# A modulation of one or two row vectors, summed on the vector engine instead of multiplied on the tensor engine

## The chip, the cores and the metric

The kernel runs on one core of a Trainium2 chip. The metric is the device time of one execution in microseconds, as the median of several runs. The engines are named as the profile names them: PE is the tensor engine (PEld its weight loads), DVE the vector engine, ACT the scalar engine, POOL the GpSimd engine, and SP issues most of the DMAs.

## The reference, cut to what matters

Two transformer blocks follow one another on 512 tokens of width 1024. The first has a hybrid mixer (dilated attention and retention), a cross attention to 256 memory tokens and a gated MLP. The second block is modulated: six vectors of width 1024 are computed from a condition vector `c`, and the same from `c_ctx` for the context tokens.

```
silu_c = jax.nn.silu(c)[:, None, :]
silu_cc = jax.nn.silu(c_ctx)
mod_x = jnp.split(silu_c @ w_mod[l] + b_mod[l], N_MOD, axis=-1)
mod_c = jnp.split(silu_cc @ w_mod[l] + b_mod[l], N_MOD, axis=-1)
h  = _modulate(_rms(x, norm_attn[l]), mod_x[0], mod_x[1])
hc = _modulate(_rms(ctx, norm_attn[l]), mod_c[0], mod_c[1])
...
x = x + mod_x[2] * _merge(...)
x = x + mod_x[5] * _sq_relu_mlp(_modulate(_rms(x, norm_mlp[l]), mod_x[3], mod_x[4]), w_mlp_in[l], w_mlp_out[l])
```

`w_mod` is 1024 x 6144 in float32, 25 MB. The product is thus two rows of 1024 times this matrix. Of `mod_c` only the first two of the six vectors are used.

## The kernel before, in words

All of it is float32. A large product is made of three products of split operands: ACT rounds a tile to its high part (`whi`, `xhi`), DVE subtracts to get the low part (`wlo`, `xlo`), and TensorE multiplies high by high, high by low and low by high (`mm3s`, lines 227 to 237).

Weights come in tiles of 512 KB (`weights`, lines 153 to 181): four row tiles of 128 by 256 columns. SP issues the load to one of two buffers `wraw` (line 172). Then `step` is called (line 175), then ACT makes `whi` (line 178) and DVE makes `wlo` (line 179), each with two buffers. A product over 1024 rows needs two such tiles, so the two buffers of `whi` and `wlo` hold just one product's weights.

`step` (lines 183 to 189) advances a generator that carries background work for the second block: one step at each weight load, and a second one at each eighth load. The generator is set in `mixer` (line 532), after the projections of the first half of the attention. It is `modulation`, 48 steps, followed by `part_ahead`, 48 steps that split columns of the second block's input weights and store them. Both load through three buffers of 4 KB a partition, named `fraw`, in the pool `fill`.

A step of `modulation` (lines 773 to 781) issues from SP the load of one row tile, 128 rows by 1024 columns, for vector j and row tile k, and then sends the products of the tile that was loaded two steps before. Such products (lines 748 to 755) are four matmuls with the two condition columns as weights, padded to 32 columns; each of the four takes 256 columns and lies in its own 32 columns of the array. They add up over eight row tiles in one PSUM bank of the tag `fl`. At the eighth tile ACT copies the bank, two transposes turn it, and DVE adds the bias to the result in `mods`, where features lie on partitions (lines 756 to 764). For vectors 2 and 5 a further transpose and an ACT DMA store the vector as a row (lines 765 to 771).

`modulation_inputs` (lines 727 to 735) loads the two condition vectors and the bias by ACT's queue and turns them by the helper `rows_T` (lines 706 to 719), each with a buffer of its own.

The steps fall beside this work of the first block: the attention (to about 200 us), the projections of the retention (200 to 265), the keys and values of the memory (`memory`, lines 579 to 602, about 265 to 350, one 512 KB tile of weights for half as much matmul work as in the projections before) and the output projection (from 350). The attention's softmax and the retention's norms need DVE, ACT and POOL.

The order on SP is that of the program. On the other engines a planner orders the instructions by program order and by when it reckons them ready; each engine then runs its list in order.

Of the kernel before, what the change touches and what calls it, by code (L numbers as in the profile page):

```python
# [10 lines left out]
F32 = mybir.dt.float32  # L11
F32R = mybir.dt.float32r
BF = mybir.dt.bfloat16
AF = mybir.ActivationFunctionType
OP = mybir.AluOpType
# [60 lines left out]
class Kernel:  # L76
# [204 lines left out]
    def turned(self, xs, t0, A, B, out, tags):  # L281

        nc = self.nc
        for k in range(8):
            pt = self.bank([128, 2, 128], tags[k % 2])
            for t in range(2):
                nc.tensor.transpose(pt[:, t], xs[t0 + t][:, k * 128:k * 128 + 128], self.ident)
            f = pt.rearrange("p a b -> p (a b)")
            to = [v[:, t0 * 128:t0 * 128 + 256] for v in out(k)]
            if B is None:  # L290
                self.split(*to, f, scale=A[:, k:k + 1])
                continue
            p2, f = f, self.page([256])
            if k % 2:
                nc.scalar.activation(f, p2, AF.Identity, scale=A[:, k:k + 1], bias=B[:, k:k + 1])
            else:
                nc.vector.tensor_scalar(f, p2, A[:, k:k + 1], B[:, k:k + 1], op0=OP.mult, op1=OP.add)
            self.split(*to, f)
# [407 lines left out]
    def rows_T(self, srcs, tag, func=None, eng=None, pool=None):  # L706

        nc = self.nc
        n = sum(k for _, k in srcs)
        r = (pool or self.tmp).tile([128, 128], F32, name="rows" + (tag if pool else "r"), bufs=1)[:n]  # L710
        i = 0
        for src, k in srcs:
            (eng or nc.sync).dma_start(r[i:i + k], bass.AP(tensor=src.tensor, offset=src.offset, ap=[[128, k], [1, 128]]))
            i += k
        if func is not None:
            nc.scalar.activation(r, r, func)
        pt = self.bank([128, n], "pt")
        nc.tensor.transpose(pt, r, self.ident[:n, :n])
        return pt
# [7 lines left out]
    def modulation_inputs(self):  # L727

        nc, ap = self.nc, self.ap
        pt = self.rows_T([(ap["c_2"], 8), (ap["c_ctx_2"], 8)], "crow", AF.Silu, nc.scalar, self.fill)  # L730
        cs = self.fill.tile([128, 8, 32], F32, name="cs")
        nc.gpsimd.memset(cs, 0.0)
        nc.vector.tensor_copy(cs[:, :, :2], pt.rearrange("p (v k) -> p k v", v=2))
        bm = self.cols([(ap["b_mod_2"], 48)], "bmod", self.fill, nc.scalar)
        self.mod_in = cs, bm

    def modulation(self):

        nc, ap = self.nc, self.ap
        cs, bm = self.mod_in
        mods = self.mods = self.const.tile([128, 48, 2], F32, name="mods")
        w = ap["w_mod_2"][0]
        self.modrow = {}
        bank = {}

        def products(j, k, raw):
            if k == 0:
                bank[0] = self.bank([128, 256], "fl")  # L750
            ps = bank[0]
            for q in range(4):
                nc.tensor.matmul(ps[32 * q:32 * q + 32], cs[:, k], raw[:, 256 * q:256 * q + 256], start=k == 0, stop=k == 7, tile_position=(0, 32 * q))
            if k < 7:
                return
            m = self.fill.tile([128, 256], F32, name="fm")
            nc.scalar.activation(m, ps, AF.Copy)
            pt = self.bank([128, 2, 4, 32], "fl")
            for f in range(2):
                nc.tensor.transpose(pt[:, f].rearrange("p a b -> p (a b)"), m[:, f * 128:f * 128 + 128], self.ident)  # L760
            mj = mods[:, 8 * j:8 * j + 8].rearrange("p (q f) v -> p f q v", f=2)
            for f in range(2):
                b = bm[:, 8 * j:8 * j + 8].rearrange("p (q f) -> p f q", f=2)[:, f, :, None].to_broadcast([128, 4, 2])
                nc.vector.tensor_tensor(mj[:, f], pt[:, f, :, :2], b, op=OP.add)
            if j in (2, 5):
                pr = self.bank([8, 128], "fl")
                nc.tensor.transpose(pr, mods[:, 8 * j:8 * j + 8, 0], self.ident)
                r = self.fill.tile([8, 128], F32, name="fr")
                nc.vector.tensor_copy(r, pr)
                d = self.modrow[j] = self.dram.tile([8, 128], F32, name=f"modrow{j}")  # L770
                nc.scalar.dma_start(d, r)

        todo = []
        for j in range(6):
            for k in range(8):
                raw = self.fill.tile([128, 2, 512], F32, name="fraw", bufs=3).rearrange("p a b -> p (a b)")
                nc.sync.dma_start(raw, w[k * 128:k * 128 + 128, j * 1024:j * 1024 + 1024])
                todo.append((j, k, raw))
                if len(todo) > 2:
                    products(*todo.pop(0))  # L780
                yield
        for t in todo:
            products(*t)

    def gain_shift(self, g, sh, sc, v, tag):

        a = self.const.tile([128, 8], F32, name=tag)
        self.nc.vector.scalar_tensor_tensor(a, self.mods[:, sc * 8:sc * 8 + 8, v], 1.0, g, op0=OP.add, op1=OP.mult)
        return a, self.mods[:, sh * 8:sh * 8 + 8, v]
# [805 lines left out]
```

## Time and profile before

| what | us |
|---|---|
| median of 3 runs (2325.2 to 2325.77) | 2325.56 |
| the profiled execution | 2328.74 |
| its span, first to last instruction | 2326.9 |
| PE busy | 2200.2 |
| DVE busy | 1210.9 |
| ACT busy | 965.2 |
| POOL busy | 275.0 |

Durations below come from the one profiled execution. A matmul's busy time is modelled from its start to the end of its pipeline, so the time from one start to the next tells what it takes from the others. A matmul of float32 that isn't split shows as two instructions. Idle time of an engine that isn't the bottleneck costs nothing. The stretches named below are cuts of the span made for this reading.

### The profile page before, as it was taken

How to read it: one execution, taken by the hardware profiler on the slowest of the kernel's cores; microseconds unless marked ns; L12 is line 12 of the kernel's file. 1: busy time of each engine (PE TensorE's matmuls, PEld its weight loads, DVE VectorE, ACT ScalarE, POOL GpSimd, SP SyncE). 2: the span in 40 equal slices, each digit the busy share in tenths (PEclk: the TensorE clock that was granted, in tenths of full speed). 3: DMA queues.
4: the chain of work that ended last, by engine and by line, in shares of the span. 5: the costliest groups of instructions: out<-in, count | busy, mean ns of one | idle time of the engine just before them, and what ended most of it. 6: DMA issues, size and time to landing. Idle time of an engine off the chain costs nothing.

```text
span 2326.9 us, 38350 instructions
## 1 busy us (share of the span) xinstructions
PE 2200.2 (95%) x15415; PEld 1954.7 (84%) x15415; DVE 1210.9 (52%) x2716; ACT 965.2 (41%) x1988; POOL 275.0 (12%) x435
## 2 busy tenths in 40 slices
PE   8999999998989999898989897999999998999999
PEld 8889978897779889777878786888898888898988
DVE  4554444555443333558686867436776354434343
ACT  4442334545333232555555553545655223313221
POOL 0221100001000001201222220202110002010112
PEclk9999999999999999999999998999999998999999
DMA  5234485465762332512121310241012542323332
GB/s 176 83 118 146 161 280 198 137 203 174 234 227 86 99 101 73 179 49 88 46 91 46 97 46 15 73 128 31 29 40 87 181 136 73 100 91 92 99 98 94
DMA packets 195817, 262.06 MB, mean 113 GB/s; under 512 B 12343, under 2 KB 157495, under 8 KB 195639
## 3 DMA queue, kind: packets, MB, share of 16 engines
q1 hardware_dynamic: 188864, 244.61, 32.7%
q10 hardware_dynamic: 6775, 15.00, 1.7%
q8 instruction: 121, 1.98, 0.3%
q14 instruction: 57, 0.47, 0.1%
HBM read 223.39 MB, written 36.18 MB: 112 GB/s over the span
## 4 chain that ended last, share of the span: by engine, by line
PE 74%; issue 9%; DVE 6%; DMA 4%; ACT 4%; POOL 3%; SPq 0%; ACTq 0%; POOLq 0%; DVEq 0%
PE pg L234 15%; PE pg L235 15%; PE pg L237 14%; PE sc L234 4%; PE sc L237 4%; PE sc L235 4%; DMA parts<-fraw 2%; DMA whi<-parts 1%; PE pg L223 1%; PE pg L224 1%; PE pg L225 1%; PE sc L1470 1%; DVE inv L1383 1%; DVE invt L1380 1%; PE pa L1148 1%
## 5 line engine op out<-in xcount | busy, mean ns | idle before, releaser
L179 DVE TENSOR_TENSOR wlo<-wraw,whi 128x1024 fp32r<-128x1024 f32 (+2 forms) x267 | 325.8, 1222 | 407.6 <-ACT whi L178 403.4
L234 PE MATMUL pg<-xhi,whi 128*128 128x512 f32 (+1 forms) x1104 | 426.6, 389 | 27.2 <-DMA whi<-parts 11.3
L178 ACT ACTIVATE whi<-wraw 128x1024 fp32r<-128x1024 f32 (+2 forms) x267 | 275.7, 1035 | 416.9 <-PE pg L235 354.4
L235 PE MATMUL pg<-xlo,whi 128*128 128x512 f32 (+1 forms) x1104 | 425.7, 388 | 0.0
L237 PE MATMUL pg<-xhi,wlo 128*128 128x512 f32 (+1 forms) x1104 | 291.3, 384 | 1.2 <-DMA wlo<-parts 1.0
L234 PEld LDWEIGHTS pg<-xhi,whi 128*128 128x128 f32 x1104 | 210.7, 191 | 73.6 <-ACT whi L178 13.2
L235 PEld LDWEIGHTS pg<-xlo,whi 128*128 128x128 f32 x1104 | 210.9, 192 | 36.7
L237 PEld LDWEIGHTS pg<-xhi,wlo 128*128 128x128 f32 x1104 | 203.1, 190 | 41.1 <-DMA wlo<-parts 2.7
L234 PE MATMUL pg<-whi,xhi 128*128 128x256 f32 (+1 forms) x608 | 158.4, 291 | 0.3 <-ACT a L980 0.3
L235 PE MATMUL pg<-whi,xlo 128*128 128x256 f32 (+1 forms) x608 | 157.2, 289 | 0.0
L234 PE MATMUL sc<-whi,a 128*128 128x256 f32 x560 | 141.5, 285 | 1.6 <-ACT whi L178 1.6
L235 PE MATMUL sc<-whi,a 128*128 128x256 f32 x560 | 141.5, 284 | 0.0
L235 PE MATMUL pg<-whi,a 128*128 128x256 f32 x560 | 140.4, 283 | 0.0
L234 PE MATMUL pg<-whi,a 128*128 128x256 f32 x560 | 140.3, 283 | 0.0
L234 PEld LDWEIGHTS pg<-whi,xhi 128*128 128x128 f32 x608 | 118.4, 195 | 4.7 <-ACT whi L178 2.7
L235 PEld LDWEIGHTS pg<-whi,xlo 128*128 128x128 f32 x608 | 118.1, 194 | 1.1 <-issue 0.8
L237 PE MATMUL pg<-wlo,xhi 128*128 128x256 f32 (+1 forms) x608 | 104.0, 289 | 12.6 <-DVE wlo L179 12.6
L929 POOL TENSOR_TENSOR a<-a,a 128x256 f32<-128x256 f32 x64 | 48.9, 763 | 514.0 <-DVE a L928 513.3
L234 PEld LDWEIGHTS sc<-whi,a 128*128 128x128 f32 x560 | 106.4, 190 | 2.1 <-ACT whi L178 1.8
L1254 DVE SCALAR_TENSOR_TENSOR a<-a,convw,a 128x511 f32<-128x511 f32 (+3 forms) x160 | 100.6, 652 | 13.8 <-ACT a L1248 12.9
L235 PEld LDWEIGHTS sc<-whi,a 128*128 128x128 f32 x560 | 106.2, 190 | 0.3
L234 PEld LDWEIGHTS pg<-whi,a 128*128 128x128 f32 x560 | 105.8, 189 | 0.2
(468 smaller groups left out, 4609.2 us busy)
## 6 DMA issues: line engine op xcount, KB each, us to landing
wraw<-in_w_in SPq DMA_DIRECT2D x56, 512.0 KB, 5.9
fraw<-in_w_mod SPq DMA_DIRECT2D x48, 512.0 KB, 5.5
parts<-fraw SPq DMA_DIRECT2D x48, 512.0 KB, 4.1
wraw<-in_w_gate_up SPq DMA_DIRECT2D x44, 512.0 KB, 4.8
wraw<-in_w_mlp_in SPq DMA_DIRECT2D x32, 512.0 KB, 3.9
wraw<-in_w_mlp_out SPq DMA_DIRECT2D x32, 512.0 KB, 3.4
whi<-parts SPq DMA_DIRECT2D x26, 512.0 KB, 3.9
wlo<-parts SPq DMA_DIRECT2D x26, 512.0 KB
```

The lines of the kernel that those rows point to most:

```text
L178: nc.scalar.activation(hi, raw, AF.Copy)
L179: self.wlo_eng.tensor_tensor(lo, raw, hi.bitcast(F32), op=OP.subtract)
L223: mm(out, a[0], b[0], start=start, stop=False)
L224: mm(out, a[0], b[1], start=False, stop=False)
L225: mm(out, a[1], b[0], start=False, stop=stop)
L234: mm(out, A[k][0], B[k][0], start=start and k == 0, stop=False)
L235: mm(out, A[k][late], B[k][1 - late], start=False, stop=False)
L237: mm(out, A[k][1 - late], B[k][late], start=False, stop=stop and k == n - 1)
L929: nc.gpsimd.tensor_tensor(self.x[t][:, cs], self.x[t][:, cs], u, op=OP.add)
L1148: nc.tensor.transpose(pt[:, s, i * 128:i * 128 + 128], p2[i][:, (2 * s2 + s) * 128:(2 * s2 + s) * 128 + 128], self.ident)
L1254: dve.scalar_tensor_tensor(y, v, wi, y, op0=OP.mult, op1=OP.add)
L1380: dve.tensor_tensor(t_, L[:, j + 1:, j:j + 1].to_broadcast([128, n, w]), Y[:, j:j + 1, b].to_broadcast([128, n, w]), op=OP.mult)
```

## The change

The modulation is computed in another way. The 6144 columns are cut into 24 units of 256. A step loads four row tiles of one unit: still 512 KB, in pieces of 1 KB. DVE multiplies each row tile by the condition's value of each row, a scalar per partition, and adds up the eight row tiles in a tile `facc` (128 by 256). The remaining sum over the 128 partitions is a matmul: `facc` gives the weights, 128 columns at a time, and a column of ones is the moving operand, so that the features come out on partitions with no transpose. The second vector is summed for the first eight units only. A step sends the sums of the tile that was loaded one step before (it was two), and the matmuls of a unit follow one step after its last sums. The rows buffers of condition, bias and a later gain are now one (`rowsf`).

```diff
-        r = (pool or self.tmp).tile([128, 128], F32, name="rows" + (tag if pool else "r"), bufs=1)[:n]
+        r = (pool or self.tmp).tile([128, 128], F32, name="rows" + ("f" if pool else "r"), bufs=1)[:n]
...
-        cs = self.fill.tile([128, 8, 32], F32, name="cs")
-        nc.gpsimd.memset(cs, 0.0)
-        nc.vector.tensor_copy(cs[:, :, :2], pt.rearrange("p (v k) -> p k v", v=2))
+        cs = self.fill.tile([128, 2, 8], F32, name="cs")
+        nc.vector.tensor_copy(cs.rearrange("p v k -> p (v k)"), pt)
+        col = self.fill.tile([128, 1], F32, name="col")
+        nc.gpsimd.memset(col, 1.0)
...
-        def products(j, k, raw):
-            if k == 0:
-                bank[0] = self.bank([128, 256], "fl")
-            ps = bank[0]
-            for q in range(4):
-                nc.tensor.matmul(ps[32 * q:32 * q + 32], cs[:, k], raw[:, 256 * q:256 * q + 256], start=k == 0, stop=k == 7, tile_position=(0, 32 * q))
-            if k < 7:
-                return
-            m = self.fill.tile([128, 256], F32, name="fm")
-            nc.scalar.activation(m, ps, AF.Copy)
-            pt = self.bank([128, 2, 4, 32], "fl")
-            for f in range(2):
-                nc.tensor.transpose(pt[:, f].rearrange("p a b -> p (a b)"), m[:, f * 128:f * 128 + 128], self.ident)
...
+        def of(u):
+            return range(2 if u < 8 else 1)
+
+        def products(u, k0, raw):
+            if k0 == 0:
+                sums[u] = [self.fill.tile([128, 256], F32, name="facc", bufs=3) for v in of(u)]
+            for k in range(k0, k0 + 4):
+                for v, acc in enumerate(sums[u]):
+                    c = cs[:, v, k:k + 1]
+                    if k == 0:
+                        nc.vector.tensor_scalar(acc, raw[:, 0], c, None, op0=OP.mult)
+                    else:
+                        nc.vector.scalar_tensor_tensor(acc, raw[:, k - k0], c, acc, op0=OP.mult, op1=OP.add)
+
+        def turned(u):
+            accs = sums.pop(u)
+            n = len(accs)
+            pt = self.bank([128, 2, n], "fl")
+            for q in range(2):
+                for v in range(n):
+                    nc.tensor.matmul(pt[:, q, v:v + 1], accs[v][:, 128 * q:128 * q + 128], col, start=True, stop=True)
+            b = bm[:, 2 * u:2 * u + 2][:, :, None].to_broadcast([128, 2, n])
+            nc.vector.tensor_tensor(mods[:, 2 * u:2 * u + 2, :n], pt, b, op=OP.add)
...
-        for j in range(6):
-            for k in range(8):
-                raw = self.fill.tile([128, 2, 512], F32, name="fraw", bufs=3).rearrange("p a b -> p (a b)")
-                nc.sync.dma_start(raw, w[k * 128:k * 128 + 128, j * 1024:j * 1024 + 1024])
-                todo.append((j, k, raw))
-                if len(todo) > 2:
-                    products(*todo.pop(0))
+        for u in range(24):
+            for k in (0, 4):
+                raw = self.fill.tile([128, 2, 512], F32, name="fraw", bufs=3).rearrange("p a (b c) -> p (a b) c", b=2)
+                src = w[k * 128:k * 128 + 512].rearrange("(k p) f -> p k f", p=128)
+                nc.sync.dma_start(raw, src[:, :, u * 256:u * 256 + 256])
+                todo.append((u, k, raw))
+                if len(todo) > 1:
+                    if k == 4 and u:
+                        turned(u - 1)
+                    products(*todo.pop(0))
                 yield
         for t in todo:
             products(*t)
+        turned(u)
```

## Rows read from the trace of the kernel before

**Rows 1.** The page: busy time of each engine, and the chain that ended last.

```profile
PE 2200.2 (95%) x15415; PEld 1954.7 (84%) x15415; DVE 1210.9 (52%) x2716; ACT 965.2 (41%) x1988; POOL 275.0 (12%) x435
...
PE 74%; issue 9%; DVE 6%; DMA 4%; ACT 4%; POOL 3%; SPq 0%; ACTq 0%; POOLq 0%; DVEq 0%
```

**Rows 2.** Busy time by stretch: stretch, length, engines (instructions), clock, DMA share, GB/s.

```profile
40.00:200.00 160.00, 158.09 (x1240) 140.27 (x1239) 78.03 (x253) 69.23 (x136) 29.62 (x52) 0.99 0.35 116
200.00:265.00 65.00, 64.45 (x558) 60.21 (x556) 30.70 (x64) 19.06 (x32) 7.59 (x12) 1.00 0.41 138
265.00:350.00 85.00, 80.24 (x692) 68.84 (x692) 43.27 (x84) 30.35 (x49) 6.92 (x12) 0.98 0.74 250
350.00:382.00 32.00, 32.00 (x279) 29.48 (x279) 11.18 (x19) 10.94 (x27) 0.00 (x0) 1.00 0.53 173
...
1047.00:1105.00 58.00, 49.41 (x571) 41.99 (x572) 49.08 (x173) 30.20 (x88) 11.26 (x20) 0.94 0.27 88
```

**Rows 3.** The products: PE, PEld by stretch; then groups (busy, mean ns | idle).

```profile
40.00:200.00 160.00, 7.88 (x104) 2.67 (x104) 0.99 0.35 116
200.00:265.00 65.00, 4.71 (x72) 1.93 (x72) 1.00 0.41 138
265.00:350.00 85.00, 12.84 (x168) 4.38 (x168) 0.98 0.74 250
350.00:382.00 32.00, 2.99 (x40) 0.89 (x40) 1.00 0.53 173
...
L753 PE MATMUL fl<-fraw,cs 128*32 128x256 f32 x384 | 28.4, 386 | 1.3 <-DMA fraw<-in_w_mod 1.3
...
L760 PE MATMUL fl<-ident,fm 128*128 128x128 f32 x12 | 2.4, 282 | 0.0
```

**Rows 4.** The timeline at a border of weight tiles: start, us, instruction.

```profile
175.17 1.23 DVE L179 TENSOR_TENSOR wlo<-wraw,whi 128x1024 fp32r<-128x1024 f32 x1 [1.97 <-ACT whi L178]
...
175.89 1.07 PE L753 MATMUL fl<-fraw,cs 128*32 128x256 f32 x16
...
176.61 1.23 DVE L179 TENSOR_TENSOR wlo<-wraw,whi 128x1024 fp32r<-128x1024 f32 x1 [0.21 <-ACT whi L178]
176.89 0.39 PE L234 MATMUL pg<-whi,xhi 128*128 128x256 f32 x1
...
177.94 0.64 PE L237 MATMUL pg<-wlo,xhi 128*128 128x256 f32 x4
```

**Rows 5.** The timeline of matmuls with one moving column, in the second block.

```profile
1565.43 0.95 PE L1044 MATMUL pt<-ones,a 128*128 128x1 f32 x8
1566.23 0.48 PE L223 MATMUL pg<-cq,whi 128*128 128x512 f32 x1
```

**Rows 6.** The timeline of the convolution's multiply-and-adds on DVE.

```profile
961.18 3.49 DVE L1254 SCALAR_TENSOR_TENSOR a<-a,convw,a 128x254 f32<-128x254 f32 x8 [0.18 <-ACT a L1248]
...
972.30 3.11 DVE L1254 SCALAR_TENSOR_TENSOR a<-a,convw,a 128x510 f32<-128x510 f32 x4 [2.33 <-ACT a L1248]
```

**Rows 7.** Waits from 40 to 382: total us, times, longest.

```profile
SPq L777 <- PE fl L753: 220.1, 23, 33.0
...
PEld fl L753 <- DMA fraw<-in_w_mod: 2.1, 2, 1.8
```

**Rows 8.** DMA issues of the page: count, KB each, median us to landing.

```profile
wraw<-in_w_in SPq DMA_DIRECT2D x56, 512.0 KB, 5.9
fraw<-in_w_mod SPq DMA_DIRECT2D x48, 512.0 KB, 5.5
```

**Rows 9.** The timeline where the bias rows are turned.

```profile
50.17 0.26 PE L718 MATMUL pt<-ident,rowsbmod 48*128 48x48 f32 x1
```

**Rows 10.** The timeline of DVE and POOL, both on tiles in SBUF.

```profile
222.27 3.33 POOL L521 TENSOR_TENSOR a<-a,a 128x128 f32<-128x128 f32 x4 [0.53 <-DVE a L520]
...
223.06 0.68 DVE L401 TENSOR_TENSOR a<-a,a 128x512 f32<-128x512 f32 x1
...
224.45 0.84 DVE L404 TENSOR_TENSOR a<-a,a 128x512 f32<-128x512 f32 x1
```

More of the change, by code (lines that the diff above doesn't have):

```diff
@@ L730, in modulation_inputs @@
         pt = self.rows_T([(ap["c_2"], 8), (ap["c_ctx_2"], 8)], "crow", AF.Silu, nc.scalar, self.fill)
-        cs = self.fill.tile([128, 8, 32], F32, name="cs")
-        nc.gpsimd.memset(cs, 0.0)
-        nc.vector.tensor_copy(cs[:, :, :2], pt.rearrange("p (v k) -> p k v", v=2))
+        cs = self.fill.tile([128, 2, 8], F32, name="cs")
+        nc.vector.tensor_copy(cs.rearrange("p v k -> p (v k)"), pt)
+        col = self.fill.tile([128, 1], F32, name="col")
+        nc.gpsimd.memset(col, 1.0)
         bm = self.cols([(ap["b_mod_2"], 48)], "bmod", self.fill, nc.scalar)
-        self.mod_in = cs, bm
+        self.mod_in = cs, col, bm
     def modulation(self):
         nc, ap = self.nc, self.ap
-        cs, bm = self.mod_in
+        cs, col, bm = self.mod_in
         mods = self.mods = self.const.tile([128, 48, 2], F32, name="mods")
@@ L745, in modulation @@
         self.modrow = {}
-        bank = {}
-        def products(j, k, raw):
-            if k == 0:
-                bank[0] = self.bank([128, 256], "fl")
-            ps = bank[0]
-            for q in range(4):
-                nc.tensor.matmul(ps[32 * q:32 * q + 32], cs[:, k], raw[:, 256 * q:256 * q + 256], start=k == 0, stop=k == 7, tile_position=(0, 32 * q))
-            if k < 7:
-                return
-            m = self.fill.tile([128, 256], F32, name="fm")
-            nc.scalar.activation(m, ps, AF.Copy)
-            pt = self.bank([128, 2, 4, 32], "fl")
-            for f in range(2):
-                nc.tensor.transpose(pt[:, f].rearrange("p a b -> p (a b)"), m[:, f * 128:f * 128 + 128], self.ident)
[L761 to L765, printed above, removed]
+        sums = {}
+        def of(u):
[19 more added lines that the diff above has]
+            nc.vector.tensor_tensor(mods[:, 2 * u:2 * u + 2, :n], pt, b, op=OP.add)
+            if u in (11, 23):
+                j = u // 4
                 pr = self.bank([8, 128], "fl")
```

## The prediction

> **What bounds the kernel now.** I read the page's totals and its chain of waits first: TensorE is busy for 95% of the span and holds 74% of the chain, so work taken off TensorE is worth its length where nothing else is late [rows 1]. The modulation lies between 40 and 382 us, so I then read busy time by stretch [rows 2]: from 40 to 265 and from 350 to 382 TensorE is busy for 254.5 of 257 us; from 265 to 350 (two projections of memory, one weight load after another) for 80.2 of 85. VectorE is at 49% (78.0 of 160), 47%, 51% and 35% in the four stretches. The products on TensorE are spread over all of them: 104, 72, 168 and 40 instructions, thus 13, 9, 21 and 5 of the 48 products of eight instructions (four calls, two instructions each: 384 for 192 calls) [rows 3].
>
> **What goes.** One product pair takes 1.00 us from its start at 175.89 to the next matmul at 176.89 [rows 4], so 0.50 us a product; the groups' busy time of 28.4 us gives 0.59 [rows 3]. I take 0.55: 48 x 0.55 = 26.4 us. The 12 transposes of the finished rows go too, 2.4 us busy [rows 3]. Their six ACT copies and twelve small VectorE additions stand on nobody's path, and 24 small additions replace them; I count nothing. Two waits of TensorE for a modulation load, 2.1 us together, go [rows 7]; VectorE can now wait for the same load instead, and I count 1 us of the 2.1.
>
> **What TensorE gets.** For each of 24 units of 256 columns, two matmuls per row vector, with 128x128 sums as weights and one moving column. Units 0 to 7 have two vectors, the rest one: 8 x 4 + 16 x 2 = 64 calls, 128 instructions. This very form is in the trace: eight such instructions run from 1565.43 to the next matmul at 1566.23, 0.10 us each [rows 5]. 128 x 0.10 = 12.8 us. Balance on TensorE: -26.4 - 2.4 + 12.8 - 1 = -17.0 us, if every part reaches the end.
>
> **What VectorE gets.** Eight row tiles times two vectors in 8 units and one in 16: 256 instructions over 128x256, 224 of them multiply-and-add onto a sum. The nearest rows are the convolution's multiply-and-adds of 254 elements: eight in 3.49 us, 0.44 each [rows 6]. Four of 510 elements that build on one another take 3.11 us, 0.78 each, with no overlap; so with one vector, where each step needs the last one's sum, I take 0.47, the 3.49 us being a mix. Two vectors alternate: 0.44. A product with two vectors costs 8 x 0.44 = 3.5 us, with one 4 x 0.47 = 1.9 us. In all 16 x 3.5 + 32 x 1.9 = 117 us more on VectorE. From 254 to 510 elements the price grows by 0.34 us, so 0.34 is what 256 elements take alone and 0.10 the rest of an instruction: if the rest were hidden, 256 x 0.34 = 87 us, the lower end; at 0.50 each it is 128, the upper.
>
> **What hides that.** By stretch, VectorE's old work plus the new [rows 2, 3]:
> 40 to 200: 78.0 + 13 x 3.5 = 123.5 of 160 us. 200 to 265: 30.7 + 3 x 3.5 + 6 x 1.9 = 52.6 of 65. 265 to 350: 43.3 + 21 x 1.9 = 83.2 of 85. 350 to 382: 11.2 + 5 x 1.9 = 20.7 of 32.
> In three stretches there is room (64 to 81%); in the third there is none. The most that VectorE reaches in a long stretch of this kernel is 49.1 of 58 us, 85%, and there TensorE too falls to 85% [rows 2]. So the third stretch is where the cover ends: TensorE's need there falls from 80.2 by 21 x 0.55 and a third of the transposes to 68, plus 10 units x 4 x 0.10 = 4, to 72 us, but it can't be shorter than VectorE's 83. I forecast that this stretch keeps its length, and that the 8 us saved there become TensorE idle time.
>
> Outside it: 27 products x 0.55 = 14.9, two thirds of the transposes 1.6, against 88 instructions x 0.10 = 8.8: -7.7, and -1 for the wait: -8.7 us. Of that something is lost at the borders between two weight tiles. There a product pair was fill: VectorE ends the first low part at 176.40 and the second at 177.84; the first is needed at 177.94 at the latest (its matmuls then began 1.05 us after 176.89) [rows 4]. Without the 1.00 us of fill, TensorE would come to it at 176.94 and to the second about 1.44 us later, at 178.4: slack of about 0.5 us each. The remaining fill of column matmuls is 0.8 us per unit with two vectors, 0.4 with one. One multiply-and-add of 0.47 us that starts just before the low part uses that slack up, a second one makes TensorE wait 0.4 us. With some 13 such borders outside the third stretch and half of them hit: +2.5 us (none to 13 x 0.5 = +6.5).
>
> **Edits near nothing.** SP issues as many loads (48) of the same size, in the same places; each now has 1 KB pieces in place of 4 KB. The weight loads have 1 KB pieces already and land after 5.9 us against 5.5 [rows 8]: 0.4 us later, hidden by three buffers; in the third stretch, with the DMAs at 0.74 of their time [rows 2], this could cost up to 2 us, which VectorE's bound hides. SP waits 220.1 us in all for products to free a modulation buffer [rows 7], with the weight loads queued behind. A product is now sent one step after its load, not two, and VectorE runs ahead of TensorE: the buffer comes free earlier, and so do the weight loads behind. That gain is bounded by TensorE's idle time of 4.8 us in the third stretch; I take none of it. The shared buffer for rows makes the bias load wait for the turn of the condition rows at 50 us; the bias was turned at 50.17 [rows 9], now about 2 to 3 us later, first needed more than 30 us later. If TensorE stands behind it: up to 2.5 us; I take 0.5. The column matmuls need sums that were sent a load step before, some 4 to 6 us; their wait I take as none, the bound is 24 x 0.47 = 11 us if each comes one multiply-and-add too early.
>
> **Sum.** -8.7 + 2.5 + 0.5 = -5.7 us. The profiled execution took 2328.74 us with a span of 2326.9, 1.84 around it; it would end at 2323.0. The median of the timed runs, 2325.56, is 3.2 us below the profiled time; less 5.7 it gives **2319.9 us**. A difference under 0.2%, some 4.7 us, can't be told from none.
>
> **A rule against it.** While POOL multiplies in 3.33 us (four instructions that read SBUF), VectorE's first 512-element operation on two SBUF inputs takes 0.68 us and the last 0.84 [rows 10]. The Trainium skill (SBUF — State Buffer, Who interferes with whom) says that a VectorE instruction with two SBUF inputs and a GpSimd instruction that reads SBUF exclude each other, the later one waiting for the whole of the first. The row agrees at most by a sixth of a microsecond, not by a whole POOL instruction of 0.83 us. As a mechanism here: POOL is busy 44 of the 342 us, so 13% of 256 instructions, 33, would wait some 0.4 us on average, +14 us of VectorE time, 9 of them between 40 and 200 where POOL's 29.6 us lie [rows 2]; VectorE there comes to 133 of 160, 83%, next to the 85% mark, the gain outside is gone and 3 us more: 2328 us. I give it 0.04.
>
> **Rivals.**
> 1. Everything reaches the end. The third stretch shrinks with TensorE, because VectorE overlaps its work better (the lower end of 0.34 leaves it at 43.3 + 21 x 4 x 0.34 = 72 of 85) and SP runs ahead: -17.0 us, 2308.6. For it: TensorE is on the chain nearly throughout [rows 1]. Against: 83 of 85 by the nearest rows. 0.17.
> 2. Nothing moves. The fill was free time: at each border TensorE waits for the low part instead of doing the product. The slack of 0.5 us at each border [rows 4] speaks against half of it, the 1.9 to 3.5 us of sums that stand in VectorE's order around these low parts for it. -8.7 shrinks to -1: 2324.6. 0.18.
> 3. Slower: VectorE becomes the bound from 265 to 350. It decides from the point at which VectorE's need passes 85% of the stretch, 72 us; it is 83. If it can't be packed closer than the 85% seen elsewhere, the stretch takes 83.2 / 0.85 = 98 us, +13; less 5.7 from outside: +7.3, 2332.9. TensorE's clock, granted at 0.94 where it is 85% busy [rows 2], is part of that mark. For it: the sum. Against: SP need not wait for TensorE any more, and sums can be put between low parts as long as the three buffers last. 0.21.
> 4. The port rule above: 0.04.
> The forecast itself, 2315 to 2323.5, has 0.40.
>
> **How the numbers follow.** About three quarters of the forecast's 0.40 lies more than 0.2% below (0.31), with rival 1: 0.48 faster. The rest of the forecast and rival 2: 0.27 the same. Rivals 3 and 4: 0.25 slower. The range runs from 2307 to 2333: it leaves out less than half of rival 1 below and half of rival 3 above, under 0.2. The unknown costs (borders none to +6.5, column waits to +11, bias to +2.5) stay inside it.
>
> **What would show it.** Right: multiply-and-adds of 0.44 to 0.5 us, 117 us in all; column matmuls at 0.10 us; VectorE over 90% between the same weight loads of the third stretch, that stretch no shorter; the three others shorter by about 2 us each. Wrong: sums under 0.4 us or over 0.55; TensorE waiting for sums at the column matmuls; low parts behind sums at most borders, with TensorE's idle time before the low part's matmuls above 10 us; SP blocked on VectorE.

## The result, and the profile after

The kernel after takes 2340.42 us, the kernel before 2325.66 on the same chip: 1.0072 times as long, 95% interval 1.0054 to 1.0090. That is slower by some 15 us, where 5.7 us less were forecast, and lies above the range. The profiled execution took 2340.87 us with a span of 2338.8.

The page of the kernel after, busy time of each engine and the chain that ended last [rows 1]:

```profile
PE 2205.5 (94%) x15147; PEld 1977.3 (85%) x15147; DVE 1309.8 (56%) x2984; ACT 963.4 (41%) x1982; POOL 283.2 (12%) x435
...
PE 72%; issue 9%; DVE 7%; ACT 4%; DMA 4%; POOL 3%; SPq 0%; POOLq 0%; ACTq 0%; DVEq 0%
```

VectorE has 98.9 us more, as was intended. But TensorE, with 268 instructions fewer, is busy 5 us longer. Some of its matmuls must have run more slowly. The groups of the new instructions from 40 to 400 us (busy, mean ns | idle time before them) show whether the new work itself was dear [rows 5, 6]:

```profile
L762 DVE SCALAR_TENSOR_TENSOR facc<-fraw,cs,facc 128x256 f32<-128x256 f32 x224 | 103.0, 480 | 8.5 <-DMA fraw<-in_w_mod 6.9
...
L760 DVE TENSOR_SCALAR facc<-fraw,cs 128x256 f32<-128x256 f32 x32 | 10.8, 347 | 6.8 <-DMA fraw<-in_w_mod 6.8
...
L770 PE MATMUL fl<-col,facc 128*128 128x1 f32 x128 | 16.9, 243 | 0.5 <-DVE facc L762 0.5
```

It was not: 113.8 us of sums by groups (VectorE's total rose by less, as neighbours overlap), and TensorE waited 0.5 us for them. Busy time by stretch of the kernel after, the cuts moved with the work (columns as in [rows 2]):

```profile
40.00:216.00 176.00, 169.69 (x1149) 154.73 (x1148) 120.61 (x370) 68.71 (x134) 35.82 (x52) 0.87 0.32 104
216.00:281.00 65.00, 63.82 (x524) 62.56 (x523) 49.07 (x115) 17.97 (x29) 7.91 (x12) 1.00 0.48 156
281.00:365.00 84.00, 73.80 (x562) 70.68 (x562) 72.04 (x161) 31.10 (x47) 7.58 (x12) 0.94 0.71 235
365.00:398.00 33.00, 33.00 (x275) 33.00 (x274) 21.35 (x43) 11.37 (x28) 0.00 (x0) 0.99 0.67 221
```

The attention takes 176 us in place of 160, with the clock granted at 0.87 in place of 0.99. By these cuts the other three stretches keep their lengths to about a microsecond. From weight load to weight load (20, 29, 45 and 50, counted from 0) they are shorter by 1.4, 0.8 and 1.7 us, and load 20 comes 18.9 us late. Now the attention finer, first the kernel before, then the kernel after, by the same columns:

```profile
60.00:80.00 20.00, 20.00 (x142) 16.89 (x140) 12.25 (x54) 11.57 (x23) 2.93 (x6) 1.00 0.05 17
160.00:180.00 20.00, 20.00 (x178) 18.19 (x179) 13.54 (x24) 6.96 (x12) 5.65 (x6) 1.00 0.45 141
```

```profile
60.00:80.00 20.00, 18.07 (x76) 14.76 (x76) 13.00 (x52) 7.10 (x16) 0.00 (x0) 0.64 0.16 52
160.00:180.00 20.00, 19.52 (x91) 17.58 (x91) 10.65 (x37) 5.07 (x11) 5.92 (x9) 0.55 0.17 54
...
60.00:64.00 4.00, 3.72 (x19) 2.39 (x18) 3.48 (x14) 2.23 (x4) 0.00 (x0) 1.00 0.00 0
64.00:68.00 4.00, 2.35 (x10) 2.23 (x11) 3.56 (x13) 1.30 (x4) 0.00 (x0) 0.69 0.27 87
68.00:72.00 4.00, 4.00 (x17) 3.66 (x18) 1.48 (x10) 1.14 (x4) 0.00 (x0) 0.50 0.51 176
...
80.00:84.00 4.00, 4.00 (x24) 3.75 (x22) 1.40 (x6) 1.15 (x3) 2.92 (x6) 0.68 0.02 4
...
156.00:160.00 4.00, 3.09 (x13) 2.38 (x14) 3.15 (x14) 1.98 (x5) 2.07 (x5) 0.71 0.01 2
160.00:164.00 4.00, 4.00 (x15) 3.23 (x15) 2.56 (x13) 1.00 (x2) 1.29 (x3) 0.50 0.01 2
...
176.00:180.00 4.00, 4.00 (x27) 4.00 (x27) 1.51 (x5) 0.83 (x2) 0.00 (x0) 0.73 0.02 5
```

At two places, from 65 to 82 and from 157 to 178 us, TensorE runs at the lower of its two clock levels (0.50 is 1.2 GHz). Between the first and last rows of each place all are at 0.50: by the rows from 64 to 84 and from 156 to 180, the clock lost is 4 x (0.31 + 3 x 0.50 + 0.32) = 8.5 us and 4 x (0.29 + 4 x 0.50 + 0.27) = 10.2 us. What TensorE did before the clock fell, in its timeline (a bracket holds the idle time before an instruction and what ended it):

```profile
63.33 0.39 PE L225 MATMUL sc<-a,a 64*128 64x512 f32 x1
65.65 0.79 PE L237 MATMUL pg<-wlo,xhi 128*128 128x256 f32 x2 [1.93 <-DVE wlo L179]
...
155.55 0.39 PE L461 MATMUL pt<-ident,a 128*128 128x128 f32 x2
156.91 0.43 PE L465 MATMUL sc<-a,a 128*128 128x64 f32 x2 [0.98 <-ACT a L463]
```

It stood waiting, the first time for a low part of weights, the second time for ACT in the attention's chain. VectorE's timeline, first two lines of the kernel before and then the kernel after, shows how late the low parts came at the two places:

```profile
56.48 1.21 DVE L179 TENSOR_TENSOR wlo<-wraw,whi 128x1024 fp32r<-128x1024 f32 x1
...
128.61 1.23 DVE L179 TENSOR_TENSOR wlo<-wraw,whi 128x1024 fp32r<-128x1024 f32 x1
```

```profile
55.77 0.60 DVE L760 TENSOR_SCALAR facc<-fraw,cs 128x256 f32<-128x256 f32 x2
56.29 0.48 DVE L762 SCALAR_TENSOR_TENSOR facc<-fraw,cs,facc 128x256 f32<-128x256 f32 x1
...
62.50 0.47 DVE L762 SCALAR_TENSOR_TENSOR facc<-fraw,cs,facc 128x256 f32<-128x256 f32 x1
...
64.37 1.22 DVE L179 TENSOR_TENSOR wlo<-wraw,whi 128x1024 fp32r<-128x1024 f32 x1
...
136.15 0.61 DVE L760 TENSOR_SCALAR facc<-fraw,cs 128x256 f32<-128x256 f32 x2
...
169.60 0.47 DVE L762 SCALAR_TENSOR_TENSOR facc<-fraw,cs,facc 128x256 f32<-128x256 f32 x1
169.99 1.22 DVE L179 TENSOR_TENSOR wlo<-wraw,whi 128x1024 fp32r<-128x1024 f32 x1
```

Count weight loads from 0. The low part of load 7 could have begun at 56, when its high part was done; the kernel before made it at 56.48. Now eight sums and the attention's own operations stand ahead of it in VectorE's list. When it has come, at 65.65, TensorE waits no more. But until 79.08 only six of the projection's matmuls stand in its list among the attention's, and the clock stays at half. Load 13 is the eighth at which the background work advances, and there `step` takes two steps: sixteen sums. They don't come one behind another: the planner has spread them among the attention's reductions, each of which waits for TensorE or ACT. So the low part, queued behind the last of the sixteen, begins 34.9 us after its high part (135.1). From 148.4 to 173.45 us TensorE has no matmul of the projection, and the attention's short chain is all but alone on it.

### The profile page after: what moved, and what is told of

The parts are those of the page before. It is cut to its first block, busy times and chain, and to the rows that moved or that the text cites. A ratio compares the mean times of both kernels' runs of the same rounds, so it can differ in the third digit from the quotient of the medians.

```text
span 2338.8 us, 38068 instructions
## 1 busy us (share of the span) xinstructions
PE 2205.5 (94%) x15147; PEld 1977.3 (85%) x15147; DVE 1309.8 (56%) x2984; ACT 963.4 (41%) x1982; POOL 283.2 (12%) x435
## 4 chain that ended last, share of the span: by engine, by line
PE 72%; issue 9%; DVE 7%; ACT 4%; DMA 4%; POOL 3%; SPq 0%; POOLq 0%; ACTq 0%; DVEq 0%
PE pg L234 14%; PE pg L235 14%; PE pg L237 14%; PE sc L234 4%; PE sc L237 4%; PE sc L235 4%; DMA whi<-parts 1%; PE pg L223 1%; PE pg L224 1%; PE pg L225 1%; PE sc L465 1%; DVE wlo L179 1%; DMA fraw<-in_w_mod 1%; DVE inv L1396 1%; DVE invt L1393 1%
## 5 line engine op out<-in xcount | busy, mean ns | idle before, releaser
L762 DVE SCALAR_TENSOR_TENSOR facc<-fraw,cs,facc 128x256 f32<-128x256 f32 x224 | 103.0, 480 | 8.5 <-DMA fraw<-in_w_mod 6.9
```

Of the source, the lines that this page charges most:

```text
L762: nc.vector.scalar_tensor_tensor(acc, raw[:, k - k0], c, acc, op0=OP.mult, op1=OP.add)
```

## The experiments

Theory 1: sums ahead of the low parts on VectorE hold back the projection, and TensorE, left with the attention's chain, falls to half its clock. Theory 2: the shared rows buffer holds TensorE at 50 us (it waited 1.8 us at line 718 for the bias rows). Theory 3: the removed products were the fill that kept TensorE's clock; VectorE is not to blame.

All runs in one table. Times are medians; a ratio is to runs of the kernel before on the same chip (their medians were 2323.3 to 2328.2). Low parts and the high part of load 16 are start times from the traces. The last column is the clock granted from 60 to 80 and from 160 to 180 us.

| kernel | us | ratio (95%) | low 7 | low 13 | high 16 | clock |
|---|---|---|---|---|---|---|
| before | 2325.66 | | 56.5 | 128.6 | 174.1 | 1.00, 1.00 |
| after | 2340.42 | 1.0072 (1.0054-1.0090) | 64.4 | 170.0 | 193.5 | 0.64, 0.55 |
| e1 step behind the split | 2322.27 | 0.9987 (0.9970-1.0004) | 55.7 | 127.1 | 171.8 | 1.00, 1.00 |
| e2 one vector | 2319.28 | 0.9972 (0.9951-0.9992) | 56.2 | 126.2 | 172.0 | 1.00, 1.00 |
| e3 own rows buffer | 2341.14 | 1.0082 (1.0050-1.0113) | 66.3 | 173.2 | 198.5 | 0.74, 0.50 |
| e6 before + sums | 2330.05 | 1.0020 (1.0001-1.0038) | 57.0 | 130.4 | 176.5 | 1.00, 1.00 |
| e7 sums a step later | 2319.90 | 0.9987 (0.9956-1.0018) | 56.2 | 143.3 | 172.7 | 1.00, 1.00 |
| e8 e6, a step earlier | 2329.92 | 1.0027 (1.0007-1.0047) | 57.0 | 127.7 | 175.6 | 1.00, 1.00 |
| e9 e1 and e7 | 2320.03 | 0.9981 (0.9963-0.9999) | 56.8 | 127.8 | 174.4 | 1.00, 1.00 |
| e10 before, step behind | 2326.09 | 0.9988 (0.9970-1.0007) | 56.0 | 127.9 | 173.4 | 1.00, 1.00 |
| e11 e1 at load 7 only | 2331.16 | 1.0017 (0.9997-1.0036) | 57.3 | 164.3 | 188.2 | 1.00, 0.67 |
| e12 e1 at load 13 only | 2332.22 | 1.0018 (1.0004-1.0032) | 65.7 | 137.6 | 185.6 | 0.68, 1.00 |
| e13 e9, additions late | 2320.18 | 0.9971 (0.9955-0.9986) | 55.9 | 126.4 | 172.6 | 1.00, 1.00 |
| e14 after + fill | 2352.39 | 1.0127 (1.0089-1.0165) | 65.8 | 163.9 | 189.2 | 1.00, 0.69 |
| e4 after, exchanged | 2338.88 | 1.0055 (1.0034-1.0076) | 55.7 | 127.0 | 170.3 | 0.91, 1.00 |
| e5 before, exchanged | 2336.25 | 1.0035 (1.0013-1.0056) | 57.0 | 126.5 | 170.3 | 1.00, 1.00 |

**e1, the step behind the split.** In the kernel after, the sums of a step are sent behind the two parts of the weight tile, not ahead of them.

```diff
-            self.step()
             hi = self.wp.tile([128, n, fn], F32R, name="whi", bufs=2)
...
             self.wlo_eng.tensor_tensor(lo, raw, hi.bitcast(F32), op=OP.subtract)
+            self.step()
```

> The changed kernel with one line moved: the background step is called behind the two instructions that split a weight tile, not ahead of them, so that the sums stand behind the low part (L179) in program order. SP's order is the same. Theory 1 (during the attention the sums stand ahead of the low parts in VectorE's list; the projections' matmuls come late, TensorE is left with the attention's chain alone and its clock falls): most of the loss goes, 2324 to 2332 us against 2340 for the changed kernel, and between 60 and 180 us the granted clock is back at 0.95 or more. Theory 2 (the wait for the bias rows in the shared buffer at 50 us, and the order that follows from it): 2338 to 2341. Theory 3 (the removed products had kept TensorE dense and its clock up; VectorE is not to blame): 2338 to 2341.

2322.27 us, a little below theory 1's bracket: the 18 us are back. VectorE still does all its sums, TensorE still has no products. By stretch, in e1 (columns as above):

```profile
60.00:80.00 20.00, 20.00 (x127) 15.82 (x127) 15.36 (x63) 10.83 (x23) 3.25 (x6) 1.00 0.11 37
...
160.00:180.00 20.00, 20.00 (x170) 20.00 (x170) 18.57 (x44) 5.51 (x10) 7.05 (x7) 1.00 0.45 141
```

VectorE is busier than in the kernel after (15.4 and 18.6 us against 13.0 and 10.7) and nothing is late: its load is not the trouble, the order of its list is.

**e10, the control.** The same edit on the kernel before.

> The kernel before with the step taken behind the split of the weight tile and nothing else: a control for the same edit on the kernel after, which brought 18 us. Theory 1 (the edit helps only because sums stood ahead of the low parts): the kernel before has no sums, nothing changes beyond 0.2%: 2321 to 2329 us. Rival (the edit is worth that by itself, because the weight loads, the high parts or the background loads come in a better order): 2308 to 2318.

2326.09 us, not to be told from the kernel before. So the edit by itself is worth nothing that shows; it needs the sums.

**e11 and e12, one place at a time.** The kernel after with the step behind the split at a single load: load 7, the second that advances the background work (2 in place of 8 in the diff, e11), or load 13 (e12).

```diff
-            self.step()
+            late = self.steps is not None and self.loads + 1 == 8
+            if not late:
+                self.step()
...
+            if late:
+                self.step()
```

> The kernel after, with the step taken behind the split at one weight load only: the second that advances the background work (load 7 counted from 0), whose low part came at 64.4 us in the kernel after and at 56.5 before. Theory 1: that low part comes at 56 to 57, the high part of load 8 at 78 to 82 in place of 92.5, and what that place cost by load 12 (7 us) comes back; the second place, load 13, stays: 2329 to 2337. If the late low parts are not the cause: as after, 2338 to 2343.

> The kernel after, with the step taken behind the split at one weight load only: the eighth that advances the background work (load 13 counted from 0), at which two steps are taken at once, so that sixteen sums stood ahead of its low part; that came at 170.0 us, 34.9 us behind its high part, and at 128.6 before. Theory 1: the low part comes within 2 us of its high part, at about 136, the clock from 160 to 180 us is full again, and the 12 to 15 us that were lost from load 13 to load 16 come back; load 7's place stays: 2324 to 2331. If the late low parts are not the cause: as after, 2338 to 2343.

2331.16 and 2332.22 us, the first as expected, the second 1 us above its bracket: each takes back about half. The clock heals at the place that was mended and at no other, e11 first and then e12:

```profile
60.00:80.00 20.00, 20.00 (x134) 16.31 (x133) 16.08 (x61) 10.76 (x22) 2.96 (x6) 1.00 0.18 60
...
160.00:180.00 20.00, 19.52 (x117) 19.10 (x117) 13.57 (x34) 7.23 (x15) 9.90 (x12) 0.67 0.17 53
```

```profile
60.00:80.00 20.00, 18.07 (x83) 14.76 (x82) 13.12 (x50) 7.31 (x14) 0.00 (x0) 0.68 0.16 53
...
160.00:180.00 20.00, 19.31 (x152) 17.68 (x150) 17.11 (x53) 8.81 (x18) 12.66 (x17) 1.00 0.29 90
```

These two runs bear out theory 1: two single instructions of 1.2 us, one behind eight sums and one behind sixteen, carry the loss.

**e7 and e9, the sums a load step later.** e7 is the kernel after with the old distance of two steps between a load and its sums, the step still ahead of the split; e9 has both edits.

```diff
-                if len(todo) > 1:
-                    if k == 4 and u:
-                        turned(u - 1)
+                if len(todo) > 2:
+                    if k == 0 and u > 1:
+                        turned(u - 2)
                     products(*todo.pop(0))
...
+        turned(u - 1)
         for t in todo:
```

> The kernel after, but a step sends the sums of the tile that was loaded two steps before, as the kernel before did with its products, and the column matmuls come a step later too. Everything else, the place of the step ahead of the weight split among it, is as after. Theory 1 (the sums stand ahead of the low parts of the first attention weights: in the kernel after the low part of the eighth weight load ends at 65.6 us against 57.7 before, and TensorE is left with the attention's chain at 0.64 of its clock): the first sums come a load later, the low part is made at about 57 again, the stretch from 60 to 80 us has its full clock, and 12 to 20 of the 14.8 us lost come back: 2319 to 2329 us. Theory 3 (the products were TensorE's fill, and without them the clock falls, whatever VectorE does): the fill is as thin as in the kernel after, 2335 to 2345.

> The kernel after with both: the step is taken behind the split of the weight tile, and the sums are sent two steps after their load. Theory 1: either alone takes the sums from ahead of the low parts of the first attention weights, so both together give little over one: 2314 to 2323 us, low parts of the first 14 loads within 3 us of the kernel before. Theory 3: as the kernel after or a few us below, 2333 to 2342 (the run with the step behind the split, 2322.3, already speaks against it).

2319.90 and 2320.03 us. Either edit is enough, both give little over one. In e7 load 13's low part is still 16.2 us behind its high part (127.1), with 7 of the 16 sums ahead of it, yet nothing is lost: a delay of that size is still covered there.

**e2, half the sums.** The kernel after with one vector in all units; it leaves out the context's shift and scale, which are set to 0.

```diff
+        nc.gpsimd.memset(mods[:, :16, 1], 0.0)
...
-            return range(2 if u < 8 else 1)
+            return range(1)
```

> The changed kernel with one sum per row tile in all 24 units: the second vector of the first eight units, the modulation of the context tokens, is left out (zeros). A step of the first 16 costs VectorE 1.8 us instead of 3.3, some 24 us less before 230 us. Theory 1: more than half of the loss of 15 us goes, 2325 to 2332 us. Theory 2: 2338 to 2341, the bias wait being the same. Theory 3: 2338 to 2342, TensorE having 32 instructions fewer.

2319.28 us, some 6 below theory 1's bracket; part of that may be the smaller work. With four sums a step in place of eight both low parts come early, in the unchanged program order: the planner put one sum ahead of each. Theory 3, as the sole cause, has now failed in e1, e2 and e7 alike: none has the products, none loses its clock at the two places.

**e3, a rows buffer for the bias alone** (theory 2).

```diff
-name="rows" + ("f" if pool else "r")
+name="rows" + ({"bmod": "b"}.get(tag, "f") if pool else "r")
```

> The changed kernel with a rows buffer of its own for the bias (condition and the later gain still share one): the bias is loaded at the start again. Theory 1: the 1.8 us of wait at 50 us go and little else, 2336 to 2339 us. Theory 2: 2325 to 2331. Theory 3: 2336 to 2339.

2341.14 us, 2 above the brackets of theories 1 and 3: the wait at line 718 is gone from the trace, the time is not. Theory 2 falls; a microsecond or two could not be told here.

**e6 and e8, the sums beside the old products.** e6 is the kernel before, with products, and 8 or 4 scratch sums a step on VectorE; e8 sends both one step after the load, not two. Both also give condition and later gain one rows buffer, which the cut leaves out.

```diff
+            acc = self.fill.tile([128, 256], F32, name="facc")
+            for i in range(8 if j < 2 else 4):
+                part = raw[:, i % 4 * 256:i % 4 * 256 + 256]
+                if i == 0:
+                    nc.vector.tensor_scalar(acc, part, bm[:, k:k + 1], None, op0=OP.mult)
+                else:
+                    nc.vector.scalar_tensor_tensor(acc, part, bm[:, k:k + 1], acc, op0=OP.mult, op1=OP.add)
```

> The kernel before, with its products on TensorE as they were, and beside them at each of the 48 products multiply-and-adds of 128x256 on VectorE into a scratch tile: eight at the first 16 products, four at the others. Nothing reads the scratch tile. TensorE's work is that of before, VectorE's close to that of the changed kernel (one chain of eight in place of two of four). Theory 1: slower than before by 10 to 25 us, 2336 to 2350, with the clock down in part of 60 to 180 us. Theory 2: 2325 to 2328. Theory 3: 2325 to 2330, as the dense products are still there.

> The kernel before with the 8 or 4 sums of each step added on VectorE as scratch (as in the earlier run, 2330.1 us), and now products and sums are sent one step after their load, not two. The products stay on TensorE. Theory 1: the sums now stand ahead of the low parts of the first attention weights as in the kernel after, the low part of the eighth load comes at 63 to 66 us, the clock falls between 60 and 80: 2338 to 2352 us. Theory 3: the fill is on TensorE as before, so nothing falls: 2326 to 2333.

2330.05 and 2329.92 us. For theory 1 I expected the loss in both; it is not there, and both lie in theory 3's ranges (e6 0.05 us above). The traces show why that is no proof for it: in both kernels the low parts of loads 7 and 13 stand ahead of nearly all sums (57.0, 130.4 and 127.7 us). At load 7 of e6 it could not be otherwise, as sums sent two steps after their load start at load 8; the rest is the planner's order. The condition that I meant to test did not occur. What they do show is the price of some 117 us of VectorE work in itself: some 5 us, with an interval that starts near none. Why the planner ordered these kernels otherwise is not settled.

**e14, fill on the kernel after.** It tells whether the fill matters where the low parts are late.

```diff
+            ps = self.bank([128, 256], "fl")
+            for q in range(4):
+                nc.tensor.matmul(ps[32 * q:32 * q + 32], self.ident[:, :32], raw[:, q], start=True, stop=True, tile_position=(0, 32 * q))
```

> The kernel after with TensorE's old load put back as scratch: at each step four matmuls of 256 columns over the loaded tile, with 32 columns of the identity as weights, into a bank that nobody reads. The sums stay as they are. Where the low parts of loads 7 and 13 come late (64.4 and 170.0 us), does the missing fill matter too? Low parts alone decide: the clock between 60 and 80 and between 160 and 180 us still falls (0.55 to 0.8), the 20 us stay lost, and the 26 us of matmuls are added where TensorE is the bound: 2352 to 2368 us. The fill was what kept TensorE's clock: the clock stays above 0.9 in both stretches, most of the 20 us comes back, and the matmuls add their 26: 2340 to 2350.

2352.39 us, at the lowest edge of what the low parts alone would give. The first place heals in part, the second doesn't, though low part 7 is as late as before (65.8). Timeline of TensorE, then the clock, in e14:

```profile
67.04 0.50 PE L237 MATMUL pg<-wlo,xhi 128*128 128x256 f32 x2 [0.70 <-DVE wlo L179]
...
152.45 0.43 PE L465 MATMUL sc<-a,a 128*128 128x64 f32 x2 [0.74 <-ACT a L463]
```

```profile
60.00:80.00 20.00, 19.30 (x134) 15.35 (x132) 16.82 (x62) 10.24 (x22) 3.44 (x6) 1.00 0.17 55
...
140.00:160.00 20.00, 19.26 (x116) 15.18 (x115) 13.63 (x56) 9.26 (x22) 7.08 (x12) 0.89 0.09 27
160.00:180.00 20.00, 19.52 (x124) 18.03 (x124) 14.02 (x35) 6.88 (x14) 10.25 (x12) 0.69 0.18 56
```

With the fill TensorE waited 0.70 us for that low part in place of 1.93, and kept its clock. The high part of load 10 is 2.2 us later than in the kernel before; in the kernel after it was 7.4. So at the first place the missing fill was part of the loss, as theory 3 has it, but only together with the late low part. At the second place the low part is late by 32.7 us, and the clock falls with the fill too.

**e4 and e5, the background work exchanged.** The column splitting first and the modulation second, in the kernel after (e4) and before (e5).

```diff
-                self.steps = itertools.chain(self.modulation(), self.part_ahead(blocks))
+                self.steps = itertools.chain(self.part_ahead(blocks), self.modulation())
```

> The kernel after with the two halves of the background work exchanged: first the splitting of columns for the second block, then the modulation. The sums then stand beside the gated MLP and the rest of the first block and not beside the attention; the column splitting (per step one ACT copy and one VectorE subtraction) stands beside the attention. Theory 1 (what is lost is lost where VectorE is in the attention's chain): the low parts of the attention wait at most for a subtraction of 1.2 us a step, most of the 20 us lost before 200 us is not lost: 2318 to 2332 us, with a clock over 0.9 in each 20 us from 40 to 200. If the sums cost the same anywhere (VectorE's 117 us as such, or the missing fill): 2337 to 2347.

> The kernel before with the two halves of the background work exchanged, the control for the same exchange in the kernel after, which lost nothing before 200 us but some 14 us between 300 and 480. If the sums lose it (they stand beside the gated MLP there): the kernel before, without sums, stays at 2321 to 2330 us. If the exchange loses it (the column splitting, with its ACT copies and VectorE subtractions, stands beside the memory's keys and values, where DMA and weight loads are already the bound): 2334 to 2346.

2338.88 and 2336.25 us: e4 lies outside theory 1's bracket and inside the other, e5 where the exchange itself loses. Until 200 us e4 loses nothing, as theory 1 has it (low part 13 at 127.0), but it is slower for other reasons. In the single profiles, by load 48 the exchange alone (e5) has lost 6.9 us and e4 9.6: from 300 to 400 us TensorE is busy for some 80 of 100 us in both. By load 54 e5 has regained it, and e4 stands at 13.5: from 400 to 440 VectorE is busy for 33.6 us of 40, against 23.7 in e5. So moving the sums is no cure. That they cost as much there is not shown: by the ratios the exchange alone brings 8 us of e4's 13, the two intervals overlap, and e4's profile is the slowest of its runs, e5's one of the fastest.

**e13, a version to beat both.** e9, and the bias addition of a unit one step after its column matmuls. In the kernel after VectorE had stood waiting there for TensorE, 18.6 us in all from 36 to 400, once for 8.0.

```diff
             pt = self.bank([128, 2, n], "fl")
...
-            b = bm[:, 2 * u:2 * u + 2][:, :, None].to_broadcast([128, 2, n])
+            banks[u] = pt
+
+        def added(u):
+            pt = banks.pop(u)
+            n = len(of(u))
+            b = bm[:, 2 * u:2 * u + 2][:, :, None].to_broadcast([128, 2, n])
...
-                    if k == 0 and u > 1:
-                        turned(u - 2)
+                    if u > 1:
+                        (added if k else turned)(u - 2)
...
+        added(u - 1)
         turned(u)
+        added(u)
```

> A version meant to beat both: the kernel after with the step behind the split at all loads, the sums two steps after their load, and the bias addition of a unit one step after its column matmuls, so that VectorE doesn't stand waiting for these (it waited 9.0 us in four places in the kernel after, the longest 8.0, with all that is queued behind). Theory 1: the balance on TensorE of -17.0 us reaches the end but for what the stretch from 265 to 350 keeps: 2310 to 2319 us. If that wait covers nothing that is late: as with the two edits alone, 2318 to 2323.

2320.18 us, 0.9971 (0.9955 to 0.9986): faster than the kernel before by some 7 us, than the kernel after by 20. It missed theory 1's 2310 to 2319. The wait is 5.2 us in place of 18.6, but it was 6.2 in e9 already, and e9's time is inside the same interval: that this third edit brings anything is not shown.

## Why the prediction was wrong

**The step that failed** is "What hides that", together with the +2.5 us for borders that was drawn from it. From 40 to 200 us it set VectorE's 123.5 us against 160 and called that room. VectorE did have that room. But an engine runs its list in order, and a low part behind eight or sixteen sums doesn't see the average. At a border I let the low part be overtaken by one or two multiply-and-adds, 0.4 us a time, +6.5 us at the most; the runs show 7.9 us later than before at load 7 and 34.9 behind the high part at load 13, and 19.5 us lost by load 16. Three things in the kernel's own text pointed at it. `step` stands ahead of the split, so all sums of a step precede the low part in program order. Each eighth load takes two steps. And the sums, sent one step after their load in place of two, reach the list before low part 7 (e7). They do not settle it, since the planner may order otherwise: with `step` in the same place the low part of load 13 has all 16 sums of its load ahead of it in the kernel after, 7 of 16 in e7 and one in e2 and e8. The list in the trace decides.

**TensorE's clock** was left out of this stretch; I used it only in rival 3. The kernel after lost 8.5 and 10.2 us of clock at its two places, nearly the whole 19.5. The sign that I had named, TensorE's idle time before the low part's matmuls, stayed small (2.5 us from 36 to 400): most of the loss was clock, not waiting. The Trainium skill (TensorE: Matmul & The Clock Gate, Part 1: The HAM clock gate) says that a hardware block sets this clock by how busy the engine has lately been. The trace agrees in so far as both falls come where TensorE is short of the projection's matmuls; that it then counts as busy for 4.00 of 4.00 us for several rows and stays at half is what this trace adds.

**What held.** TensorE's balance: -17.0 us forecast, and its busy time falls by 16.3 us in e1 and 18.4 in e7. The size of what reaches the end: -5.7 us forecast, and by the ratios some 3 in e1 and e7, 4.4 in e9 and 6.7 in e13, of which only the last two are clear of none. That e7, e9 and e13 come to 2319.9, 2320.0 and 2320.2 us, the forecast time, is partly luck: on their chips the kernel before took 2323.3 and 2326.6 us, not the 2325.56 from which the forecast starts. The price of the sums: 117 us forecast, 98.9 net and 113.8 by groups, at a mean of 0.48 us (multiply-and-add) and 0.35 (first product). The column matmuls: 0.10 us each forecast, 0.11 from start to start (eight from 100.73 us on), and a wait for sums of 0.5 us in all. The bias wait was 1.8 us against 0.5 with a bound of 2.5, and e3, without it, is no faster.

**The third stretch** kept its length in the kernel after (84 us against 85, TensorE idle for 10), as forecast, but not for the reason given. VectorE's need was to be 83.2 us, over 90% of the stretch; it was 72.0, 86%. And that the stretch can't be shorter was not borne out. From the first to the last matmul of memory's projections it took 75.5 us before, 76.4 after and 76.7 in e1, but 72.4 in e7 and 74 in e9 and e13. The profiles of e1 and e7, in windows over about the same work, differ in the clock:

```profile
259.00:344.00 85.00, 74.54 (x562) 70.53 (x560) 71.93 (x161) 32.00 (x48) 7.30 (x12) 0.94 0.67 220
```

```profile
259.00:339.00 80.00, 71.11 (x563) 67.29 (x563) 69.53 (x158) 30.91 (x47) 7.57 (x12) 1.00 0.71 232
```

In e7 VectorE is at 87%, so the 85% that I took for its most is not a bound either. What decides the clock there, and with it some 4 us, stays open.

**The rivals.** Slower it was, but by none of mine. Rival 3 put VectorE's bound in the stretch with the least room; the loss came in the one with 23% to spare. Rival 2 saw the right mechanism, low parts behind sums, and stopped at a loss of all the gain, 2324.6: it had no way to fall below nothing, since it lacked the clock and the double step. Rival 4 would have made the sums longer by 14 us of waits; they were shorter than forecast.

**Left open.** From load 132 to load 144, in the second block, where no kernel here differs, single profiles took 456 to 467 us, 464.0 in the kernel before and 459.4 after. So of the 16 us by which the profile after is late at load 132 some 4 come back without a cause in the change, and differences of 5 us between two single profiles prove nothing. Open too is why the planner put the sums ahead of the low parts in the kernel after and behind them in e2, e6 and e8.

## What to carry to other kernels

Free time on an engine is not cover; the place in its list is. For each instruction added to an in-order engine, look up which instruction with a deadline is queued behind it, in program order and then in the list that was built, count all that a step can send at once (the rare double step too), and send background work behind the urgent work of the same step. Work removed from TensorE may have been what bridged a late operand: where that is possible, reckon a late operand not at the wait that it brings, but at the stretch of half clock that can follow while the large matmuls are missing.

## What was not expected of the hardware

A wait of 1.93 us on TensorE was followed by about 17 us, and one of 0.98 us by about 21, in which it ran at 0.50 of its clock, though by its busy time it was hardly idle. The wait's length doesn't decide it. Waits of 0.70 us (e14 at 67 us) and of 0.54 (e1 at 123) were not followed by that, one of 0.74 (e14 at 152) was. In e3 the clock fell at 151 us though no wait from 134 us on was over 0.3:

```profile
148.00:150.00 2.00, 1.86 (x11) 1.33 (x11) 1.83 (x6) 1.09 (x3) 1.90 (x3) 1.00 0.00 0
150.00:152.00 2.00, 2.00 (x10) 1.34 (x9) 1.67 (x10) 1.18 (x3) 1.03 (x3) 0.78 0.08 20
152.00:154.00 2.00, 2.00 (x9) 1.55 (x9) 0.31 (x3) 0.00 (x0) 0.00 (x0) 0.50 0.75 246
```

And the wait of 1.79 us for the bias rows in the kernel after, nearly as long as that of 1.93, was followed by half clock only until about 55 us:

```profile
51.02 0.23 PE L718 MATMUL pt<-ident,rowsf 48*128 48x48 f32 x1 [1.79 <-DMA rowsf<-in_b_mod]
```

```profile
52.00:54.00 2.00, 2.00 (x8) 1.74 (x9) 2.00 (x3) 0.47 (x1) 0.00 (x0) 0.50 0.01 2
54.00:56.00 2.00, 2.00 (x14) 2.00 (x13) 1.89 (x4) 1.47 (x2) 0.00 (x0) 0.68 0.25 47
56.00:58.00 2.00, 2.00 (x20) 2.00 (x20) 1.45 (x5) 1.27 (x3) 0.00 (x0) 1.00 0.88 298
```

There the projection's matmuls went on at 54.1 us; in the two long stretches they were all but missing until shortly before the clock rose. That is an observation of single profiles, not a rule.

And some 117 us of additions on VectorE beside the old products cost some 5 us only (e6), as long as hardly any stood ahead of the low parts.
